# A two-layer hybrid mixer on one core: projection stage's affine steps on another engine, attention's column sums beside its value products, window masks in one format, and the end of layer 0

## The chip, the cores and the metric

The kernel runs on one core of one Trainium2 chip. The time is the device time of one execution in microseconds (us). Before the change it was 2352.65 us, the median of 3 runs (2346.26 to 2353.32).

The engines are named as in the profile: PE is the matrix engine (PEld is its weight loading), DVE the vector engine, ACT the scalar (activation) engine, POOL the general SIMD engine, SP the queue engine that issues most DMA transfers. A "q" behind a name (ACTq, SPq) means the engine's sequencer, for instance when it issues a transfer.

## The reference

Two layers. Each takes 512 latent tokens and 256 context tokens of width 1024, makes one normalised, modulated input `h`, and runs three mixers on it whose outputs are gated and merged:

```
mod = silu(c) @ ada_w + ada_b                     # shift, scale, gate
h = rms_norm(x, norm_g) * (1 + scale) + shift
za, ga, zb, gb, zc, gc, zg = split(h @ w_in)      # 1024 -> 7680 columns, "projection"
# 1. RWKV-7, two directions
z = token_shift(za);  r, k, v, wd, ad = split(z)
decay = exp(-exp(w_log)),  a = sigmoid(a0 + ad @ a_up)
kk = normalised(k * k_k);  k_dir = k * (1 + (a - 1) * k_a)
S <- S diag(w) - (S kk)(kk*a)^T + v k^T;  y = S r # scan over tokens
# 2. latent attention (MLA), dense, 8 heads of 96;  3. windowed GQA, 8 heads of 64,
#    keys within +-128 positions and all context keys, a sink in the softmax
m = sum_n sigmoid(zg_n) * ((y_n * silu(g_n)) @ w_branch_out[n])
x = x + gate * (m @ w_out)
```

The context tokens go through the same layer; of the last layer only the latent output is wanted.

## The kernel before, in words

Everything is float32. A large product is done as three PE products of rounded halves ("fp32r", high and low part of the weights and of the input): `wh*hh`, `wh*hl`, `wl*hh`. The helper `split_w` (L160 to L166) loads four 128x128 weight tiles, makes `wh` on ACT (L165) and `wl` on POOL (L166). Attention's scores use fp32r too; its value products (`yps`, `ypc`), its column sums (`sps`) and the transposed maxima (`mxp`) are plain float32 products, which the trace shows as two instructions each. The window's masks are bf16 products of an identity with a matrix of zeros and large negative numbers, accumulated onto the scores.

A list scheduler sets each engine's order when the kernel is built, by priority bands; the band `SERVE` goes first. A pool hands out on-chip places; a tile that takes a place waits until the last user of that place has ended. Each engine, and each DMA queue, works its list strictly in order.

Per layer the stages follow one another, with projections (`g<-hh,wh` and its two companions) spread as filler between the instructions of the later stages:

- *Projection stage* (`zphase`, about 70 to 300 us in layer 0 and 1400 to 1600 in layer 1). It makes RWKV's inputs. Its main loop has four steps `p` of 128 channels. A step projects `rT` and `vT` (gemms into `gc` and `g`, then a token shift: ACT L352, DVE L353 and L355), reverses `vT` on POOL (L439), transposes it on PE, does two small products whose tanh comes from ACT (L461), and then for both directions `d`: an affine step on `th` (POOL, L466), a running sum (DVE scan, L468), two exponentials (`Ep` L472 and `Em` L475 on ACT, one place for `Em`), an affine step for `kd` (POOL, L478), and ten multiplications into `ar` and `bk` on DVE (L479 to L490). At the end of the step `ks` gets the second direction's `kd` added (POOL, L499). The products `pr<-ar,bk` of a step (`inside`, copied out on ACT at L411) come on PE in the next step, after the next `rT` and `vT` gemms. `ada`, the modulation for later, runs beside it (`modps` on PE from `ada_w` tiles).
- *RWKV scan* with its inverses (300 to 700 us).
- *MLA heads* (about 780 to 960) and *GQA heads* (1010 to 1160 in layer 0). `turns` lets the preparation of one head run beside the attention of the head before. `together` (L857) takes the probability tiles in batches of three and issues their value products; `normalise` (L896) copies the value sum out (ACT, L900), makes the column sums `sps` on PE, and then the reciprocal and the product on DVE. `max_rows` (L873) transposes a head's row maxima (`mxp`).
- *End of the layer*. `gate_out`, called by `gated`, (its transfers are L795, its product L799) loads a gate tile `gt`, multiplies and stores to `ygd`; `branch` (L1334) loads `ygt` from `ygd`, splits it into `yh`/`yl` and multiplies by `w_branch_out`.

Of the kernel before, what the change touches and what calls it, by code (L numbers as in the profile page):

```python
# [60 lines left out]
def build(tc, A, out):  # L61
# [36 lines left out]
    kbias = cpool.tile([P, 3], F32, name="kbias")  # L98
# [3 lines left out]
    b_eps, b_gn, b_kk = kbias[:, 0:1], kbias[:, 1:2], kbias[:, 2:3]  # L102


    win = cpool.tile([P, 3, P], BF16, name="win")
    V.tensor_copy(win[:, 0], ident)
    G.memset(win[:, 1:3], 0.0)
    G.affine_select(win[:, 1], win[:, 1], [[1, P]], ALU.is_ge, NEG, base=0, channel_multiplier=-1)
    G.affine_select(win[:, 2], win[:, 2], [[-1, P]], ALU.is_ge, NEG, base=0, channel_multiplier=1)
# [114 lines left out]
    def ada(l, pp, mod, parts, pool=None):  # L224
# [6 lines left out]
        def bank(shape, name):  # L231
            if pool:
                return rps.tile(shape, F32, tag="c", name=name, bufs=CB)
            return gps.tile(shape, F32, tag="m", name=name, bufs=1)
# [15 lines left out]
        for q, h in [(q, h) for q in parts for h in range(512 // n)]:  # L250
            ps = bank([P, n], "modps")
# [11 lines left out]
            pt = bank([P, nf, 2], "modpt")  # L263
# [79 lines left out]
    def zphase(l, D, hh, hl, last, DL, ready, pace):  # L343
# [18 lines left out]
        with tc.tile_pool(name="zp", bufs=1, reuse_waits="tile") as rp:  # L362
# [36 lines left out]

            def inside():  # L400
# [22 lines left out]
            for p in range(4):  # L423
# [39 lines left out]
                for d in range(2):  # L463

                    th, tha = ths[d], thas[d]
                    G.tensor_scalar(th, th, 0.5, 0.5, ALU.mult, ALU.add)  # L466
                    cum = tmp()
                    V.tensor_tensor_scan(cum, chunk, th, 0.0, ALU.mult, ALU.add)  # L468
                    Ep = big("Ep", [P, NCH, 65], 2)
                    G.memset(Ep[:, :, 0:1], 1.0)  # L470
# [7 lines left out]
                    G.tensor_scalar(kd, tha, c1("ka1"), c1("ka0"), ALU.mult, ALU.add)  # L478
# [19 lines left out]
                    if d:  # L498
                        G.tensor_tensor(ks, ks, kd, ALU.add)  # L499
# [357 lines left out]
    def together(late, values, begins, rest=False):  # L857


        while len(late) >= (1 if rest else EB - 3):  # L860
            some = [late.pop(0) for _ in range(min(len(late), 3))][::-1]
            with band(SERVE), in_line():
                for x in sorted(some, key=lambda x: not begins(*x)):
                    values(*x)

# [5 lines left out]

    def max_rows(mx, r0, nt, row, out, floor=None):
# [3 lines left out]
        mm(ps[rows], mx, ident)  # L876
# [18 lines left out]
    def normalise(ap, yps, acc, n, y, sink=None):  # L895
# [24 lines left out]
    def weigh(o, v, e, c0, first, done):  # L920
# [119 lines left out]
    def mla_heads(l, last, ap, qt, kt, vh, scale, tq0, filler):  # L1040
# [7 lines left out]
        heads, ys, later, late, sums = {}, {}, [], [], {}  # L1048

        def values(hd, k, s0, n, e, acc, y):  # L1050
# [4 lines left out]
            if i == nk - 1:  # L1055
                later.append(normalise(ap, sums.pop((hd, s0))[0], acc[:, s0 - qo:s0 + n - qo], n,
                                       y[:, hd % 2, (s0 - qo) // 2:(s0 + n - qo) // 2]))
                next(later[-1])
                if s0 and hd % 2:
                    later.append(gated(ap, l, 4 + hd // 2, y, segs))  # L1060

        def prepare(hd):
# [25 lines left out]
            max_rows(mx[:, 0, tq0:6], 96, nt, row, qh[xr])  # L1088
            heads[hd] = kh, kl, qh, ql

        def attend(hd):
# [7 lines left out]
            for s0, n, k in [(s0, n, k) for s0, n in segs[::-1] for k in range(6 if s0 else 2)]:  # L1099
# [6 lines left out]
                together(late, values, lambda *x: True)  # L1106
                if s0:
                    yield
            if hd == 7:
                together(late, values, lambda *x: True, True)  # L1110
# [113 lines left out]
    def gqa_heads(l, F, last, ap, KA, KB, vh, sink8, queries, xs, filler):  # L1224
# [8 lines left out]
        ys, sinks, later, qs_, late, sums = {}, {}, [], {}, [], {}  # L1233

        def values(hd, k, g0, s0, e, acc, y):
# [4 lines left out]
            if i == nk - 1:  # L1240
                later.append(normalise(ap, sums.pop((hd, g0))[0], acc[:, g0 - qo:g0 + n - qo], n,
                                       y[:, hd % 2, (g0 - qo) // 2:(g0 + n - qo) // 2],
# [418 lines left out]
```

## Time and profile before

| | us |
|---|---|
| median of 3 runs | 2352.65 |
| profiled execution | 2353.25 |
| its span, first to last instruction | 2351.5 |
| outside the span | 1.75 |
| mean granted PE clock | 0.950 of full |

The profiled execution lies 0.6 us above the median. Sums below are made against its 2353.25. The rows are shown under a heading of their own further down. In a row of a timeline the columns are start, duration, engine, line and operation, output<-inputs, and in brackets the idle time of the engine just before with what ended it. A matrix instruction's duration is longer than its distance to the next one, since they overlap: what an instruction costs is read from one start to the next start.

### The profile page before, as it was taken

To read this page: it belongs to the slowest core of one execution; us is meant where nothing else is said; L and a number is where in the kernel's file an instruction comes from. 1 tells how busy PE (TensorE), PEld (TensorE's weight loads), DVE (VectorE), ACT (ScalarE), POOL (GpSimd) and SP (SyncE) were. 2 spreads that over 40 slices of the span, in tenths; PEclk is the share of its full clock that TensorE was granted. 3 is DMA by queue.
4 is the path that set the end of the run, shared out by engine and by line. 5 is a ranking of instruction groups with operands and counts; after the bars stand their busy time and mean duration, and the time that the engine had idled before them with its cause. 6 is when DMAs were issued, how large, how long until landed. Compare 5 with 4: busy or idle time off the path is not lost. (4 is left out here: it accounts for less than half of the span.)

```text
span 2351.5 us, 42314 instructions
## 1 busy us (share of the span) xinstructions
PE 2096.9 (89%) x16680; PEld 1623.2 (69%) x16680; DVE 1267.4 (54%) x2300; ACT 890.7 (38%) x1654; POOL 865.6 (37%) x699
## 2 busy tenths in 40 slices
PE   6986898888989999989699998889878998999989
PEld 3865676776877766766478876668657876666657
DVE  4476315547436666337537255742668357565643
ACT  3543212233346333354232245433333455534422
POOL 1355312111122344444362324554211145455663
PEclk9998899898999999999899999999989998999999
DMA  7146566554242111431173413566554262215344
GB/s 254 59 137 185 174 201 200 131 144 127 85 132 75 57 41 52 155 121 46 51 238 126 146 61 92 162 201 189 147 127 122 74 215 82 82 50 188 104 156 140
DMA packets 321223, 301.63 MB, mean 128 GB/s; under 512 B 111744, under 2 KB 234368, under 8 KB 321024
## 3 DMA queue, kind: packets, MB, share of 16 engines
q1 hardware_dynamic: 303216, 269.29, 38.3%
q10 hardware_dynamic: 17808, 29.63, 3.9%
q8 instruction: 132, 2.16, 0.4%
q14 instruction: 67, 0.55, 0.1%
HBM read 207.34 MB, written 91.49 MB: 127 GB/s over the span
## 5 line engine op out<-in xcount | busy, mean ns | idle before, releaser
L166 POOL TENSOR_TENSOR wl<-wf,wh 128x512 fp32r<-128x512 f32 x316 | 423.7, 1342 | 999.9 <-ACT wh L165 915.9
L154 PE MATMUL g<-hh,wh 128*128 128x512 f32 (+1 forms) x1264 | 469.2, 372 | 14.5 <-DVE st L782 6.3
L154 PE MATMUL g<-hh,wl 128*128 128x512 f32 (+1 forms) x1264 | 456.1, 361 | 4.1 <-POOL wl L166 4.0
L154 PE MATMUL g<-hl,wh 128*128 128x512 f32 (+1 forms) x1264 | 455.0, 360 | 0.0
L165 ACT CAST wh<-wf 128x512 fp32r<-128x512 f32 x316 | 195.2, 619 | 447.4 <-PE g L154 216.3
L154 PEld LDWEIGHTS g<-hh,wh 128*128 128x128 f32 x1264 | 248.9, 197 | 63.2 <-issue 10.8
L154 PEld LDWEIGHTS g<-hh,wl 128*128 128x128 f32 x1264 | 249.0, 197 | 43.6 <-issue 7.6
L154 PEld LDWEIGHTS g<-hl,wh 128*128 128x128 f32 x1264 | 249.2, 197 | 37.0 <-issue 8.8
L892 POOL TENSOR_TENSOR acc<-acc,pe 128x512 f32<-128x512 f32 (+2 forms) x128 | 145.2, 1135 | 118.0 <-ACT pe L888 98.6
L888 ACT ACTIVATE pe<-stp 128x256 f32<-128x256 f32 (+2 forms) x224 | 114.5, 522 | 190.4 <-PE stp L154 180.2
L870 DVE TENSOR_REDUCE mx<-mps 128x1 f32<-128x384 f32 (+2 forms) x256 | 124.8, 533 | 60.8 <-PE mps L154 60.1
L154 PE MATMUL g<-yh,wh 128*128 128x512 f32 (+1 forms) x224 | 79.3, 357 | 21.4 <-ACT yh L1345 17.7
L154 PE MATMUL yps<-pe,vh 128*64 128x256 f32 (+1 forms) x704 | 95.8, 381 | 1.3 <-ACT tb L900 1.2
L912 DVE RECIPROCAL rec<-sps 128x256 f32<-128x256 f32 (+1 forms) x48 | 70.3, 1478 | 35.3 <-PE sps L154 35.1
L645 DVE TENSOR_TENSOR AR<-scps,cst 64x256 f32<-64x256 f32 x96 | 40.1, 418 | 88.6 <-PE scps L154 87.4
L892 POOL TENSOR_TENSOR acc<-pe 128x512 f32<-128x512 f32 (+1 forms) x48 | 53.2, 1109 | 89.8 <-ACT pe L888 84.3
L154 PE MATMUL g<-yl,wh 128*128 128x512 f32 (+1 forms) x224 | 80.8, 361 | 5.7 <-POOL yl L1346 5.7
L154 PE MATMUL gc<-hh,wh 128*128 128x512 f32 x192 | 76.8, 400 | 8.7 <-ACT hh L325 4.6
L154 PE MATMUL g<-yh,wl 128*128 128x512 f32 (+1 forms) x224 | 79.0, 356 | 0.0
L154 PE MATMUL gc<-hl,wh 128*128 128x512 f32 x192 | 78.1, 407 | 0.1
L154 PE MATMUL scps<-AR,BK 64*128 64x128 f32 (+1 forms) x768 | 63.0, 291 | 15.8 <-DMA AR<-ard 13.5
L679 DVE TENSOR_TENSOR inv<-inv,YB 128x30 f32<-128x30 f32 (+9 forms) x180 | 70.2, 390 | 10.7 <-issue 5.1
(388 smaller groups left out, 4352.6 us busy)
## 6 DMA issues: line engine op xcount, KB each, us to landing
wf<-w_in SPq DMA_DIRECT2D x163, 256.0 KB, 2.9
wf<-ada_w SPq DMA_DIRECT2D x84, 256.0 KB, 4.2
wf<-w_in ACTq DMA_DIRECT2D x77, 256.0 KB, 3.0
bkd<-bk SPq DMA_DIRECT2D x16, 768.0 KB, 6.4
zt<-thzg SPq DMA_DIRECT2D x48, 256.0 KB, 3.1
wf<-w_bo SPq DMA_DIRECT2D x40, 256.0 KB, 2.8
thzg<-st SPq DMA_DIRECT2D x24, 384.0 KB, 2.4
vd<-t SPq DMA_DIRECT2D x64, 96.0 KB, 2.4
```

Of the source, the lines that this page charges most:

```text
L154: queued(TE.matmul(o, l, r, start=start, stop=stop, **kw))
L165: S.copy(wh, w32)
L166: eng.tensor_tensor(wl, w32, wh.bitcast(F32), ALU.subtract)
L645: V.tensor_tensor(AR[oth, pds, 2 * par, :], ps[oth, :, a0:a0 + 64], msk("ms", oth), ALU.mult)
L679: V.tensor_tensor(t3, M3[:, j:j + 1, 0:j].to_broadcast([P, n, j]), YK[:, j + 1:32, j:j + 1].to_broadcast([P, n, j]), ALU.mult)
L870: V.tensor_reduce(mx, ps, AX.X, ALU.max)
L888: S.activation(e, st, AF.Exp, scale=scale)
L892: G.tensor_tensor(acc, keep.pop(0, acc), e, ALU.add)
L912: V.reciprocal(rec, sps)
```

## The change

Six parts.

1. The window's masks become fp32r: two matrices, the identity and one triangle `far`; the other triangle comes from exchanging the two operands. The mask product stays 128x128.
2. `ada` takes one PSUM bank in two halves for its `modps`, and the small transposed product `pt` goes into the same place that the row came from.
3. `zphase`: both affine steps (`th`, `kd`) go from POOL to ACT, the add `ks+kd` from POOL to DVE. The two `Ep` tiles are made once, with their column of ones.
4. Attention: `normalise` stops once more before its reciprocal; the column sums `sps` are issued right behind the next batch of value products (`due`, `close`).
5. `max_rows` multiplies fp32r tiles: the maxima are copied into the last columns of a zeroed tile (`mr`), so that the product has 70 to 102 columns of which the first are zero.
6. `branch` takes its first `ygt` tile before `yh`/`yl`, which in layer 0 have two tags instead of two places of one tag.

```diff
-    win = cpool.tile([P, 3, P], BF16, name="win")
+    win = cpool.tile([P, 2, P], F32R, name="win")
+    identr = win[:, 0]
...
+    windows = {True: (identr, win[:, 1]), False: (win[:, 1], identr)}
...
-                            mm(w[...], win[:, 0], win[:, 1 if k < t else 2],
+                            mm(w[...], *windows[k < t], start=False,
...
         def bank(i):
             if pool:
                 return rps.tile([P, n], F32, tag="c", name="modps", bufs=CB)
+            if not m2:
+                m2.append(gps.tile([P, 512], F32, tag="m", name="modps", bufs=1))
+            return m2[0][:, 256 * (i % 2):256 * (i % 2) + n]
...
-            pt = bank([P, nf, 2], "modpt")
+            pt = ps[:, 0:2 * nf].rearrange("p (f c) -> p f c", c=2)
...
-                    G.tensor_scalar(th, th, 0.5, 0.5, ALU.mult, ALU.add)
+                    S.activation(th, th, AF.Identity, bias=b_half, scale=0.5)
...
-                    Ep = big("Ep", [P, NCH, 65], 2)
-                    G.memset(Ep[:, :, 0:1], 1.0)
+                    Ep = Eps[d]
...
-                    G.tensor_scalar(kd, tha, c1("ka1"), c1("ka0"), ALU.mult, ALU.add)
+                    S.activation(kd, tha, AF.Identity, bias=c1("ka0"), scale=c1("ka1"))
...
-                        G.tensor_tensor(ks, ks, kd, ALU.add)
+                        V.tensor_tensor(ks, ks, kd, ALU.add)
...
-    def together(late, values, begins, rest=False):
+    def together(late, values, begins, due, later, rest=False):
+        def close(ended):
+            for x in ended:
+                next(x[0])
+            later.extend(y for x in ended for y in x)
         while len(late) >= (1 if rest else EB - 3):
+            ended = due[:]
+            due.clear()
             some = [late.pop(0) for _ in range(min(len(late), 3))][::-1]
             with band(SERVE), in_line():
                 for x in sorted(some, key=lambda x: not begins(*x)):
                     values(*x)
+                close(ended)
...
+    def max_columns(ap, r0, nt):
+        mrs = [ap.tile([P, r0 + nt], F32R, name=f"mr{i}") for i in range(2)]
+        for mr in mrs:
+            S.activation(mr, ones[:, 0:1].to_broadcast([P, r0 + nt]), AF.Copy, scale=0.0)
+        return mrs
+    def rounded(mr, mx):
+        V.tensor_copy(mr[:, mr.shape[1] - mx.shape[1]:], mx)
+        return mr
...
-        mm(ps[rows], mx, ident)
+        mm(ps[0:r0 + nt], mx, identr)
...
+        yield
         rec = ap.tile([P, 256], F32, tag="rec", name="rec", bufs=2)[:, 0:h]
...
             if i == nk - 1:
-                later.append(normalise(...))
-                next(later[-1])
+                norm = normalise(...)
+                next(norm)
+                due.append([norm] + ([gated(...)] if s0 and hd % 2 else []))
...
+        yts = [tp.tile([P, 512], F32, tag="ygt", name="ygt", bufs=2 if l else 4)]
-        yh, yl = ({s0: tp.tile([P, 4, n], F32R, tag=f"{t}{s0}", name=t, bufs=1 if l else 2) for (s0, n) in segs}
+        yh, yl = ({s0: tp.tile([P, 4, n], F32R, tag=f"{t}{s0}{0 if l else n_ % 2}", name=t, bufs=1) for (s0, n) in segs}
```

What the change does to the order is seen on two engines. On POOL, in layer 0's projection stage, the list of before has between one `vT` reversal (L439) and the next the two `th` steps (L466), the two `kd` steps (L478), the small fills of `Ep` and the add (L499), with the weight splits `wl` (L166) among them:

```order
L439 TENSOR_SCALAR t_1649<-vT 128x256
L466 TENSOR_SCALAR t_1683<-t_1683 128x768
L466 TENSOR_SCALAR t_1684<-t_1684 128x768
L478 TENSOR_SCALAR ks<-t_1685,der 128x768
L478 TENSOR_SCALAR t_1744<-t_1686,der 128x768
L166 TENSOR_TENSOR wl<-wf,wh 128x512
L470 MEMSET Ep 128x12
L499 TENSOR_TENSOR ks<-ks,t_1744 128x768
L166 TENSOR_TENSOR wl<-wf,wh 128x512
L470 MEMSET Ep 128x12
L166 TENSOR_TENSOR wl<-wf,wh 128x512 x2
L439 TENSOR_SCALAR t_1972<-vT 128x512
```

The same stretch of POOL's list after the change, and some rows on to both sides:

```order
L451 TENSOR_SCALAR t_1322<-vT 128x256
L169 TENSOR_TENSOR wl<-wf,wh 128x512 x4
L451 TENSOR_SCALAR t_1641<-vT 128x512
L451 TENSOR_SCALAR t_1641<-vT 128x256
L169 TENSOR_TENSOR wl<-wf,wh 128x512 x4
L451 TENSOR_SCALAR t_1960<-vT 128x512
```

Only the reversals and the weight splits are left on POOL.

ACT's list in that stage, one step of before (`Ep` is L472, `Em` L475, the token shift's first part L352, weight halves `wh` L165):

```order
L472 ACTIVATE Ep<-t_1389 128x12x64
L475 ACTIVATE Em<-t_1389 128x768
L472 ACTIVATE Ep<-t_1413 128x12x64
L165 CAST wh<-wf 128x512
L162 DMA wf<-w_in 128x512
L352 ACTIVATE rT<-g,der 128x256
L475 ACTIVATE Em<-t_1413 128x768
L165 CAST wh<-wf 128x512
L352 ACTIVATE rT<-gc,der 128x512
L246 DMA wf<-ada_w 128x2x256 x2
```

and the same of after (`th` step L478, `Ep` L483, `Em` L486, `kd` step L489, shift L360, weight halves L168):

```order
L483 ACTIVATE Ep_858<-t_1385 128x12x64
L168 CAST wh<-wf 128x512
L486 ACTIVATE Em<-t_1385 128x768
L165 DMA wf<-w_in 128x512
L489 ACTIVATE ks<-t_1358,der 128x768
L478 ACTIVATE t_1357<-t_1357,kbias 128x768
L168 CAST wh<-wf 128x512
L360 ACTIVATE rT<-gc,der 128x512
L360 ACTIVATE rT<-g,der 128x256
L254 DMA wf<-ada_w 128x2x256
L489 ACTIVATE t_1413<-t_1359,der 128x768
L483 ACTIVATE Ep_859<-t_1407 128x12x64
```

The second direction's `Ep` now stands behind the next step's two `rT` copies, which wait for PE's gemms; before, it stood right behind the first direction's `Em`, and the second direction's `Em` between the two copies.

On PE, near the end of layer 0's GQA heads, before (`sps` are the column sums, `stp` the scores, `win` the masks):

```order
L154 MATMUL yps<-pe,vh 64x256 x2
L154 MATMUL ypc<-pe,vh 64x128 x4
L154 MATMUL mxp<-cst,mx 6x128
L154 MATMUL stp<-QA_8719,KA 128x384
L154 MATMUL stp<-QB,KB 128x384
L154 MATMUL sps<-acc,cst 64x256 x2
L154 MATMUL sps<-er,cst 64x128 x4
L154 MATMUL sps<-acc,cst 64x128 x2
L154 MATMUL sps<-er,cst 64x128 x2
L154 LDWEIGHTS win
L154 MATMUL stp<-win 128x128
```

and the same place after:

```order
L157 MATMUL yps<-pe,vh 64x256 x2
L157 MATMUL ypc<-pe,vh 64x128 x4
L157 MATMUL sps<-acc,cst 64x256 x2
L157 MATMUL sps<-er,cst 64x128 x4
L157 MATMUL mxp<-win,mr_8692 70x128
L157 MATMUL stp<-QA_8685,KA 128x384
L157 MATMUL stp<-QB,KB 128x384
L157 MATMUL stp<-win 128x128 x2
```

The float32 products now stand in one run, and the masks have no weight load of their own in the list.

## Rows read from the trace of the kernel before

**Rows 1.** The page's busy time of each engine, share of the span, instructions.

```profile
PE 2096.9 (89%) x16680; PEld 1623.2 (69%) x16680; DVE 1267.4 (54%) x2300; ACT 890.7 (38%) x1654; POOL 865.6 (37%) x699
```

**Rows 2.** Windows: start:end, length, each engine's busy us, granted clock, DMA share, GB/s.

```profile
120.00:300.00 180.00, 145.00 (x1078) 108.99 (x1079) 101.55 (x150) 60.37 (x113) 80.62 (x51) 0.89 0.57 168
1420.00:1600.00 180.00, 149.41 (x1059) 114.86 (x1059) 101.64 (x128) 78.41 (x135) 93.45 (x66) 0.92 0.55 161
960.00:1160.00 200.00, 184.68 (x1220) 134.56 (x1218) 103.96 (x189) 91.15 (x204) 87.99 (x89) 0.99 0.31 96
```

**Rows 3.** Groups by line, 120 to 300 us: busy us, mean ns | idle before, releaser.

```profile
L468 DVE TENSOR_TENSOR_SCAN t<-chunk,t 128x768 f32<-128x768 f32 x8 | 15.6, 1982 | 21.5 <-POOL t L466 21.5
...
L479 DVE TENSOR_TENSOR t<-t,kT 128x768 f32<-128x768 f32 x4 | 3.8, 946 | 0.0
...
L472 ACT ACTIVATE Ep<-t 128x768 f32<-128x768 f32 x8 | 6.8, 848 | 6.4 <-POOL wl L166 4.6 <-DVE t L468 1.6
```

**Rows 4.** One line's instructions: the add L499; durations in ns, minimum/median/maximum.

```profile
L499 POOL TENSOR_TENSOR ks<-ks,t x8: 2449/5890/6219, 144.6 to 1565.0; 128x768 f32<-128x768 f32 x8
```

**Rows 5.** Timeline, layer 0, step 2 of the projection stage, all engines.

```profile
170.80 1.99 POOL L166 TENSOR_TENSOR wl<-wf,wh 128x512 fp32r<-128x512 f32 x1
171.57 1.77 DVE L485 TENSOR_TENSOR ar<-kkn,Ep 128x512 f32<-128x512 f32 x1
...
177.52 6.20 POOL L499 TENSOR_TENSOR ks<-ks,t 128x768 f32<-128x768 f32 x1 [1.52 <-DVE t L479]
...
178.23 0.68 DVE L485 TENSOR_TENSOR ar<-kkn,Ep 128x512 f32<-128x512 f32 x1
...
183.68 1.26 POOL L166 TENSOR_TENSOR wl<-wf,wh 128x512 fp32r<-128x512 f32 x1
...
189.66 1.07 PE L154 MATMUL modps<-wf,sc 128*32 128x256 f32 x4 [12.20 <-DMA wf<-ada_w]
```

**Rows 6.** Timeline of PE: two more of its gaps in the projection stages.

```profile
238.47 0.80 PE L154 MATMUL pr<-ar,bk 64*64 64x64 f32 x10 [8.15 <-ACT t L411]
...
1468.07 1.23 PE L154 MATMUL pr<-ar,bk 64*64 64x64 f32 x18 [6.93 <-DVE bk L488]
```

**Rows 7.** What the tile `modps` waited for on PE: us, times.

```profile
  DVE mod L272: 6.8, 4
```

**Rows 8.** Timeline of PE in layer 0's GQA heads.

```profile
1141.31 0.28 PE L154 MATMUL mps<-win 128*128 128x128 bf16 x2
...
1141.99 0.23 PE L154 MATMUL mps<-win 128*128 128x128 bf16 x1
1142.03 0.37 PE L154 MATMUL stp<-QA,KA 128*128 128x256 f32 x1
1142.23 0.28 PE L154 MATMUL stp<-QB,KB 128*128 128x256 f32 x1
1142.36 0.23 PE L154 MATMUL stp<-win 128*128 128x128 bf16 x1
...
1143.54 0.38 PE L154 MATMUL mxp<-cst,mx 128*6 128x128 f32 x2
1143.85 0.45 PE L154 MATMUL stp<-QA,KA 128*128 128x384 f32 x1
1144.14 0.34 PE L154 MATMUL stp<-QB,KB 128*128 128x384 f32 x1
1144.40 0.65 PE L154 MATMUL sps<-acc,cst 128*64 128x256 f32 x4
```

**Rows 9.** Groups of PE's weight loads by form, 960 to 1160 us.

```profile
L154 PEld LDWEIGHTS stp<-QB,KB 128*128 128x128 f32 x64 | 12.3, 192 | 0.2
...
L154 PEld LDWEIGHTS <-win 128*128 128x128 bf16 x96 | 6.8, 97 | 6.2 <-issue 3.4
```

**Rows 10.** Timeline of SP's queue at layer 0's end.

```profile
1171.14 1.24 SPq L795 DMA_DIRECT2D ygd<-gt  x2
1173.90 1.76 SPq L1344 DMA_DIRECT2D ygt<-ygd  x4
```

More of the change, by code (lines that the diff above doesn't have):

```diff
@@ L97, in build @@
     ident, bones, ones = C["ident"], C["bones"], C["ones"]
-    kbias = cpool.tile([P, 3], F32, name="kbias")
+    kbias = cpool.tile([P, 4], F32, name="kbias")
     V.memset(kbias[:, 0:1], EPS)
@@ L229, in ada, with bank @@
         n = 512 if pool else 256
-        def bank(shape, name):
+        m2 = []
+        def bank(i):
             if pool:
-                return rps.tile(shape, F32, tag="c", name=name, bufs=CB)
-            return gps.tile(shape, F32, tag="m", name=name, bufs=1)
+                return rps.tile([P, n], F32, tag="c", name="modps", bufs=CB)
+            if not m2:
+                m2.append(gps.tile([P, 512], F32, tag="m", name="modps", bufs=1))
+            return m2[0][:, 256 * (i % 2):256 * (i % 2) + n]
         def four(q, h, k0):
@@ L248, in four @@
             return [ws[i // 2][:, i % 2] for i in range(4)]
-        for q, h in [(q, h) for q in parts for h in range(512 // n)]:
-            ps = bank([P, n], "modps")
+        for i_, (q, h) in enumerate((q, h) for q in parts for h in range(512 // n)):
+            ps = bank(i_)
             for k0 in range(0, KT, 4):
@@ L398, in zphase @@
             late, sums = [], []
+            Eps = [big(f"Ep{d}", [P, NCH, 65]) for d in range(2)]
+            for Ep in Eps:
+                G.memset(Ep[:, :, 0:1], 1.0)
             def inside():
@@ L864, in together @@
                     values(*x)
+                close(ended)
+        if rest:
+            with in_line():
+                close(due)
+            due.clear()
     def max_tile():
@@ L1047, in mla_heads @@
             S.copy(kh[xr, :], ones[xr, 0:1].to_broadcast([nt, T]))
-        heads, ys, later, late, sums = {}, {}, [], [], {}
+        mrs = max_columns(ap, 96, nt)
+        heads, ys, later, late, sums, due = {}, {}, [], [], {}, []
         def values(hd, k, s0, n, e, acc, y):
@@ L1105, in attend @@
                 late.append((hd, k, s0, n, probs(ap, st, n, scale, acc[:, sl], k, keep, EB), acc, y))
-                together(late, values, lambda *x: True)
+                together(late, values, lambda *x: True, due, later)
                 if s0:
@@ L1109, in attend @@
             if hd == 7:
-                together(late, values, lambda *x: True, True)
+                together(late, values, lambda *x: True, due, later, True)
         turns(8, prepare, attend, later, filler)
@@ L1232, in gqa_heads @@
         segs = (LAT,) if last else (LAT, CTX)
-        ys, sinks, later, qs_, late, sums = {}, {}, [], {}, [], {}
+        mrs = max_columns(ap, 64, nt)
+        ys, sinks, later, qs_, late, sums, due = {}, {}, [], {}, [], {}, []
         def values(hd, k, g0, s0, e, acc, y):
@@ L1240, in values @@
             if i == nk - 1:
-                later.append(normalise(ap, sums.pop((hd, g0))[0], acc[:, g0 - qo:g0 + n - qo], n,
-                                       y[:, hd % 2, (g0 - qo) // 2:(g0 + n - qo) // 2],
-                                       (sinks[hd][xr], xr, xr.start - tq0 + g0 // P)))
-                next(later[-1])
-                if g0 and hd % 2:
-                    later.append(gated(ap, l, 8 + hd // 2, y, segs))
+                norm = normalise(ap, sums.pop((hd, g0))[0], acc[:, g0 - qo:g0 + n - qo], n,
+                                 y[:, hd % 2, (g0 - qo) // 2:(g0 + n - qo) // 2],
+                                 (sinks[hd][xr], xr, xr.start - tq0 + g0 // P))
+                next(norm)
+                due.append([norm] + ([gated(ap, l, 8 + hd // 2, y, segs)] if g0 and hd % 2 else []))
         def begins(hd, k, g0, *_):
@@ L1317, in attend @@
                 st = rps.tile([P, 512], F32, tag="r", name="stp", bufs=RB)[:, 0:n]
-                edges = [(t * P - s0, 1 if t < k else 2) for t in range(s0 // P, s1 // P) if t != k] if k >= 2 else []
+                edges = [(t * P - s0, windows[t < k]) for t in range(s0 // P, s1 // P) if t != k] if k >= 2 else []
                 mm(st, KA[:, kv, ks], QA[:, s0 - qo:s1 - qo], stop=False, skip_group_check=bool(edges))
@@ L1321, in attend @@
                 for e, (o_, w) in enumerate(edges):
-                    mm(st[:, o_:o_ + P], win[:, 0], win[:, w], start=False, stop=(e == len(edges) - 1),
+                    mm(st[:, o_:o_ + P], *w, start=False, stop=(e == len(edges) - 1),
                        skip_group_check=True)
                 late.append((hd, k, g0, s0, probs(ap, st, n, scale, acc[:, s0 - qo:s1 - qo], k, keep, EB), acc, y))
-                together(late, values, begins)
+                together(late, values, begins, due, later)
                 if g0:
```

31 lines of the change are left out of this document (16 added, 15 removed).

## The prediction, made before the changed kernel ran

> **What bounds the kernel now.** I read the page's busy times first: PE is busy for 2096.9 us, 89% of the span, DVE for 54%, ACT and POOL for under 40% [rows 1]. So where PE is full, an edit is worth what it takes off PE, and where PE idles, what shortens the chain that PE waits for. The windows tell the two kinds of stage apart [rows 2]: in the GQA stage PE is busy for 184.68 of 200 us at a granted clock of 0.99, while in the two projection stages it is busy for 145.00 and 149.41 of 180 us, at 0.89 and 0.92. These two hold 35.0 + 30.6 = 65.6 us of PE idle time, and the first, third and fourth part of the change fall on the one kind or the other. Then I read, in the idle stages, the timeline around PE's gaps, and in the full ones the distances from one PE start to the next.
>
> **Projection stage (parts 2 and 3).** Removed from POOL: 16 `th` steps, 16 `kd` steps, 8 adds. Added: 32 ACT instructions of 768 columns, which I price by the exponential of the same size, 0.85 us [rows 3], 27 us in all, and 8 DVE adds at the 0.95 us of the product of that size [rows 3], 7.6 us. POOL's add took 2.4 to 6.2 us, 5.9 in the median [rows 4].
>
> ACT's 27 us cost nothing as such: it is busy for 60.37 of the 180 us in layer 0 [rows 2]. In the chain an affine step on ACT stands where one on POOL stood. The adds are another matter, because of what is queued behind them. At 177.52 POOL begins the add, which lasts 6.20 us. The weight split `wl` behind it in POOL's list starts only at 183.68; it gives a staging place free, ACT's queue issues the `ada_w` load when it has ended, and PE, which waits for that load, has stood for 12.20 us when it goes on at 189.66 [rows 5]. After the change POOL has nothing between two reversals of `vT` but weight splits, so the split can start where the add did. That takes 6.2 us out of this chain and puts 0.95 in (the DVE add): 5.2. The next step of layer 0 has the same long add, and its PE gap of 8.15 us ends with an ACT copy that waits in the same list [rows 6]; I count 5.2 again. Together 10.4.
>
> In the other six steps the add is shorter or nobody waits for it; PE's gap of 6.93 us in layer 1 ends with DVE's `bk` [rows 6], that is with the chain on DVE. That chain is stretched while POOL works: one and the same 512-column product took 1.77 us beside a POOL split and 0.68 beside the add [rows 5], 1.1 us apart. The scan waits 21.5 us in layer 0 for POOL's `th` step [rows 3], but most of that is the tanh before it, which stays. I take 1.1 for the stretch and 1.1 for the wait on `kd` and the second stretched product of a step, less 0.95 for the new add: 1.3 us a step, 8 for six. Sum for the stage: 18. Its ends are 0, if ACT's longer list delays the second direction as much as POOL is relieved, and the whole 65.6 of idle time.
>
> On this the Trainium skill has a rule (SBUF — State Buffer, "Who interferes with whom"): DVE and POOL share a pair of ports as an exclusive lock, and the loser waits for the whole instruction of the other. The 1.77 us agree with it: the POOL split began at 170.80 and lasted 1.99, to 172.79, and 0.68 later is 173.47, where the product ended at 173.34 [rows 5]. By that rule the weight splits, which stay on POOL, go on blocking DVE, and now start earlier in the step, while DVE works on `ar` and `bk`; the 1.1 of the stretch would not come back, and the stage would give 10.4 + 6 x 0.2 = 11.6 instead of 18.
>
> `ada`: PE waited 6.8 us for the `mod` addition before it could begin the next `modps` [rows 7]. With halves of a bank it need not. Most of that time PE then waits for the next load instead; I take 2, between 0 and 6.8.
>
> **Attention (parts 1, 4, 5).** First the order. Scores are fp32r, sums and values float32, and every passage from one to the other costs PE time that the starts show: a 256-column score product has the next start 0.13 behind it, unrounded about 0.12, so one of 384 columns should take 0.18; the one followed by `sps` takes 0.26, and the one that follows `mxp` 0.29, some 0.09 more for a passage in either direction [rows 8]. Counted in the two lists, the attention stages of both layers have 276 passages before and 176 after, since sums, values and `mxp` now stand in one run. 100 x 0.09 = 9 us off PE, where PE is full. That the reciprocal and the product come later costs nothing as long as the next head covers them; the order leaves a batch at least.
>
> `mxp` as float32 takes two instructions, 0.31 us to the next start, passage included [rows 8], 0.22 without; as one fp32r instruction 0.11 to 0.22. 32 of them: 0 to 3.5 saved; I take 3. The 32 small DVE copies stand before it and lie beside scores.
>
> The masks: 192 products of 128 columns, 64 alone and 64 pairs. In bf16 the mask costs PE little: after it the next product starts 0.04 later and that one lasts 0.20 instead of 0.13, 0.12 for a mask with its return to fp32r [rows 8]; two in a row last 0.28 where one lasts 0.23, so the second of a pair starts 0.05 to 0.065 behind the first. What an fp32r product of under 256 columns costs no row of before shows. From below, it is the 256 columns' 0.13 at most halved; but the weights must be loaded, and an fp32r load of 128 columns lasts 192 ns against 97 for bf16 [rows 9], and no fp32r product with its load follows another closer than the 0.12 of those with 256 columns. So 0.12 each: nothing for those alone, 0.055 for each pair, +3.5 us. From above, it is the float32 price, 0.213 for 128 columns (the 0.22 of `mxp`): 64 x 0.095 + 64 x 0.243 = +21.7; and if it were also to pay the passage both ways, 128 x 0.19 = 24 more, +45.7. I take +3.5, since the rows nearest to it are fp32r products, whose price goes with columns down to the load.
>
> The Trainium skill speaks against the masks' new format (TensorE: Matmul & The Clock Gate, "Weight-path perf modes"): the fast weight load is on for 128 weights of a type that isn't FP32. The loads' 97 against 192 ns agree [rows 9]. By that rule alone each mask pays the longer load in full where nothing covers it, 192 x 0.095 = 18 instead of 3.5, and the whole would come to 2337.
>
> Attention in sum: -9 - 3 + 3.5 = -8.5.
>
> **Layer 0's end (part 6).** The last two stores are issued from 1171.14 for 1.24 us, to 1172.38, but the `ygt` loads behind them in SP's list only at 1173.90 [rows 10]: the first of them has the place of `gt`, so it waits for the stores to land. In the list of after it waits for PE alone and can go 1.52 earlier: -1.5. They stay behind these stores in SP's list, so the long wait of PE there (from the ping-pong of one `gt` tile) stays.
>
> **Sum.** -18 - 2 - 8.5 - 1.5 = -30 from the profiled 2353.25, 2323.25; the median lies 0.6 lower: 2323.
>
> **Rivals.**
> (a) An fp32r product of 128 columns costs as much as float32: masks +21.7, `mxp` 0. Attention +12.7, in all -9: 2344. For it speaks that the kernel has no such product under 256 columns; against it that price went with columns in all forms seen.
> (b) ACT takes POOL's place. The second direction's `Ep` stands behind two `rT` copies that wait for PE's gemms of the next step (the orders show it); the stage gains nothing: -12, 2341. For it: DVE had its scan's result used at once before. Against: ACT idles for two thirds of the stage [rows 2], and `wl` comes earlier, thus the gemms too.
> (c) Slower: each mask group pays the float32 price and the passage both ways, in GQA's scores, +45.7 against -30.5 of all the rest (`mxp` 0): +15, 2368. It decides from 30.5/128 = 0.24 us for a group above today's price, where nothing is left of the gain.
> (d) The end of layer 0 is not moved, or is later: in SP's new list a gate store that waits for ACT stands among the `gt` transfers; +3, about one of the store-to-load distances there (1171.14 to 1173.90 [rows 10]), instead of -1.5: 2327.
>
> **How the numbers follow.** The forecast 0.50, (a) 0.20, (b) 0.15, (c) 0.10, (d) 0.05. The forecast's own range is 2304 (the projection stages give half of their idle time back, 33) to 2338. The range that should hold 8 in 10 goes from 2300 to 2354: it holds (a), (b) and (d) and leaves (c) out. A difference of under 0.3%, 7 us, can't be told from none here. Faster by more: 0.95 of the forecast and (d), half of (a), 0.75 of (b): 0.73. The rest of (a) and (b) is no change, with a little of the forecast, 0.13; (c) and what I may have missed, 0.14.
>
> **What would show it.** Right: PE busy in the two projection windows at over 155 of 180 us, no gap of 12 us before `modps`, no POOL work there but splits and reversals; in GQA the mask 0.11 to 0.13 from start to start, and no 0.09 before `sps`; `ygt` issued within 1.5 us of the last store. Wrong: masks 0.2 apart (then (a) or (c)), PE's gaps in the projection stage ending with ACT's `Ep` (then (b)).

## The result, and the profile after

The changed kernel took 2327.84 us (median of 4 runs, 2322.13 to 2331.07), beside 2350.17 for the kernel before, 22 us less by these medians. The ratio is 0.9885, 95% interval 0.986 to 0.9911, which is 27 us. Run again later beside the experiments, on a chip where the kernel before took 2357.17, it took 2327.81, a ratio of 0.9881 (0.986 to 0.9901). So it is faster by 22 to 29 us; 2323, 30 less, was forecast. The sum came out near, partly because errors of its terms cancel.

A table of stages, each from one PE start to another in the profiled executions, the last one to PE's end (us):

| from ... to | before | after | after, again |
|---|---|---|---|
| start ... last `pr<-ks`, layer 0 | 288.0 | 284.6 | 285.8 |
| of it the loop, from the first `pr<-twd` | 161.7 | 151.2 | 151.0 |
| RWKV, to the first MLA score | 496.9 | 498.7 | 497.9 |
| MLA, GQA, end of layer 0, to the first `g<-yh` | 392.6 | 378.3 | 377.2 |
| branch, head, projection of layer 1 | 414.5 | 409.2 | 408.0 |
| of it the loop | 148.6 | 141.6 | 141.6 |
| RWKV, layer 1 | 422.6 | 418.8 | 421.5 |
| MLA, GQA, tail of layer 1 | 333.3 | 330.9 | 332.2 |

The two last columns are the same kernel, and its stages differ by up to 3 us. Among the runs below the spread is wider. Nine runs have the same PE list in layer 0's loop and nearly the same in layer 1's; the loops took 145.7 to 151.2 us and 140.5 to 145.2 in them. RWKV differs by up to 8 with nearly the same list. So nothing under 7 us is read from one stage of one run alone. Both loops together lost 17.5 us, 18 was forecast for the stage. But layer 0's loop begins 7 us later than before (133.3 against 126.3), and attention lost 16.7 where 10 were forecast with the end of layer 0.

The page's busy line [rows 1]:

```profile
PE 2080.5 (90%) x16648; PEld 1631.0 (70%) x16648; DVE 1271.3 (55%) x2342; ACT 920.2 (40%) x1694; POOL 787.7 (34%) x646
```

POOL lost 78 us; ACT gained 30, where 27 were priced; PE lost 16. The windows of [rows 2], the same stretches of time:

```profile
120.00:300.00 180.00, 149.66 (x1111) 112.49 (x1110) 103.57 (x160) 80.78 (x138) 42.50 (x27) 0.91 0.58 174
1420.00:1600.00 180.00, 155.66 (x1115) 119.75 (x1114) 95.94 (x133) 86.95 (x153) 63.39 (x44) 0.96 0.63 180
960.00:1160.00 200.00, 170.54 (x1143) 132.32 (x1143) 109.96 (x200) 84.98 (x194) 81.79 (x80) 0.95 0.29 92
```

PE is busier in both projection stages, though the sign that the prediction gave, over 155 of 180 us, holds in the second alone. POOL works half as long in the first. The third window now holds the idle end of the layer, which begins earlier. What became of the gap of 12.20 us [rows 5] and of that of 8.15 [rows 6], in the timeline of PE:

```profile
184.91 0.63 PE L157 MATMUL modps<-wf,sc 128*32 128x256 f32 x4 [1.46 <-DMA wf<-ada_w]
190.96 0.62 PE L157 MATMUL modps<-wf,sc 128*32 128x256 f32 x4 [1.95 <-DMA wf<-ada_w]
...
199.58 0.64 PE L157 MATMUL modps<-wf,sc 128*32 128x256 f32 x2 [3.06 <-DMA wf<-ada_w]
...
235.92 1.12 PE L157 MATMUL pr<-ar,bk 64*64 64x64 f32 x16 [6.48 <-ACT t L423]
...
271.83 1.07 PE L157 MATMUL modps<-wf,sc 128*32 128x256 f32 x4 [5.50 <-DMA wf<-ada_w]
```

The loop's waits for `ada_w` are now four short ones, 12.0 us together; before they were three, 13.3 together, with the long one among them. Step 2, which had the long one, has three of the four with 6.5 us, so 5.7 less; the fourth, 5.50, is in the last step. The gap of 8.15 is now 6.48. In GQA the place of [rows 8]:

```profile
1124.24 0.33 PE L157 MATMUL mps<-win 128*128 128x128 f32 x2
1124.41 0.45 PE L157 MATMUL mps<-KB,QB 128*128 128x256 f32 x2
1124.70 0.22 PE L157 MATMUL mps<-win 128*128 128x128 f32 x1
1124.76 0.33 PE L157 MATMUL stp<-QA,KA 128*128 128x256 f32 x1
1124.93 0.28 PE L157 MATMUL stp<-QB,KB 128*128 128x256 f32 x1
1125.05 0.22 PE L157 MATMUL stp<-win 128*128 128x128 f32 x1
1125.26 0.65 PE L157 MATMUL yps<-pe,vh 128*64 128x256 f32 x4
1125.74 0.61 PE L157 MATMUL ypc<-pe,vh 128*64 128x128 f32 x8
1126.18 0.60 PE L157 MATMUL sps<-acc,cst 128*64 128x256 f32 x4
1126.71 0.65 PE L157 MATMUL sps<-er,cst 6*64 6x128 f32 x8
1127.46 0.25 PE L157 MATMUL mxp<-win,mr 128*70 128x128 f32 x1
1127.55 0.39 PE L157 MATMUL stp<-QA,KA 128*128 128x384 f32 x1
```

Values, sums and maxima stand in one run. A mask alone has the next start 0.06 behind it and that product takes 0.17, 0.23 together (0.24 in bf16 [rows 8]); a pair takes 0.17 to the next start, and the two 256-column products behind it 0.29 where two take 0.24. The first of the two behind the pair takes 0.17 as well: part of a mask's price shows in the product behind it, in both formats. Neither the float32 price nor a passage is paid: rivals (a) and (c) are out by these rows alone. The transposed maxima take 0.09 instead of 0.31.

The weight loads, by form [rows 9]; the masks' are now as long as the scores':

```profile
L157 PEld LDWEIGHTS stp<-QB,KB 128*128 128x128 f32 x64 | 12.2, 190 | 0.4 <-issue 0.3
L157 PEld LDWEIGHTS mps<-win 128*128 128x128 f32 x48 | 8.8, 188 | 0.1
```

And SP's queue at the end of layer 0 [rows 10]:

```profile
1156.39 1.24 SPq L806 DMA_DIRECT2D ygd<-gt  x2
1157.67 2.03 SPq L1386 DMA_DIRECT2D ygt<-ygd  x4
```

The loads start 1.28 behind the stores and not 2.76: the 1.5 of the forecast, to the tenth.

### The profile page after: what moved, and what is told of

It is laid out like the page before. It is cut to its first block, busy times and chain, and to the rows that moved or that the text cites. A ratio compares the mean times of both kernels' runs of the same rounds, so it can differ in the third digit from the quotient of the medians.

```text
span 2324.2 us, 42281 instructions
## 1 busy us (share of the span) xinstructions
PE 2080.5 (90%) x16648; PEld 1631.0 (70%) x16648; DVE 1271.3 (55%) x2342; ACT 920.2 (40%) x1694; POOL 787.7 (34%) x646
## 5 line engine op out<-in xcount | busy, mean ns | idle before, releaser
L169 POOL TENSOR_TENSOR wl<-wf,wh 128x512 fp32r<-128x512 f32 x316 | 439.7, 1393 | 1129.4 <-ACT wh L168 1068.6
L168 ACT CAST wh<-wf 128x512 fp32r<-128x512 f32 x316 | 195.1, 619 | 422.2 <-PE g L157 190.0
L157 PEld LDWEIGHTS g<-hh,wh 128*128 128x128 f32 x1264 | 249.8, 198 | 59.2 <-issue 10.4
L157 PE MATMUL gc<-hh,wh 128*128 128x512 f32 x192 | 78.9, 411 | 10.1 <-DVE rT L363 5.6
L157 PE MATMUL gc<-hh,wl 128*128 128x512 f32 x192 | 76.5, 399 | 0.0
```

The lines of the kernel that those rows point to most:

```text
L157: queued(TE.matmul(o, l, r, start=start, stop=stop, **kw))
L168: S.copy(wh, w32)
L169: eng.tensor_tensor(wl, w32, wh.bitcast(F32), ALU.subtract)
```

## The experiments

All ratios are to the kernel before, timed on the same chip; the changed kernel's own is 0.9881 to 0.9885. Edits are shown against the changed kernel.

**The head's banks.** The table shows that layer 0's loop begins late, and the PE list of the head has its modulation products in single pieces. Timeline of PE before, in the head, the first batches (columns as before; an instruction count of 2 is one float32 product):

```profile
36.82 1.91 PE L154 MATMUL modps<-wf,sc 128*32 128x512 f32 x12
...
39.76 1.04 PE L154 MATMUL modps<-wf,sc 128*32 128x512 f32 x2
```

and after:

```profile
35.67 1.04 PE L157 MATMUL modps<-wf,sc 128*32 128x512 f32 x2
...
37.78 1.05 PE L157 MATMUL modps<-wf,sc 128*32 128x512 f32 x2
...
40.44 1.05 PE L157 MATMUL modps<-wf,sc 128*32 128x512 f32 x4
```

Each of the four products of a batch writes a quarter of the rows (128*32); alone one takes 1.04 us, six in a row 1.91. Two kernels test this.

```diff
-            pt = ps[:, 0:2 * nf].rearrange("p (f c) -> p f c", c=2)
+            pt = (rps.tile([P, nf, 2], F32, tag="c", name="modpt", bufs=CB) if pool else
+                  ps[:, 0:2 * nf].rearrange("p (f c) -> p f c", c=2))
```

> The changed kernel with one thing undone: in the head of layer 0, where the modulation products have 512 columns, the small transposed product has a bank of its own again. Theory: with both in one bank the modulation products come free earlier, each goes as its own weights land, and what were runs of four that overlap on PE become single ones; that is why their PE time in the head rose from 14.9 us (9 runs) to 21.4 us (16 runs). Undone, they take about 15 us again, the first step of the projection stage's loop begins some 6 us earlier (at 127 instead of 133 us), and the whole comes to about 2322. Rival: the head's order was changed by something else (the Ep tiles, the masks' set-up); then the runs stay 16 and the time 2328.

2320.22 us, ratio 0.9853 (0.9831 to 0.9875). The products took 15.1 us of PE from start to next start in 9 runs (before 14.9 in 9, after 21.4 in 16), and the loop began at 128.2. In the second the batch is issued last weights first:

```diff
-                    for i in range(4):
+                    for i in reversed(range(4)):
                         mm(ps[32 * i:32 * i + 32], sc2[:, k0 + i, :], ws[i], start=(k0 == 0), stop=(k0 + 4 == KT),
```

> The changed kernel, and in the modulation product the four products of a batch are issued last first, so that the first of them waits for the weights that land last and the other three follow at once. Theory (overlap of the four is what counts): all runs in the head are of four, PE time of these products 14 us or less instead of 21.4, whole time 2321. Rival (PE waits for the weights anyway, and what counts is when they land): the head stays as long, or a batch that waits holds back the projections behind it, time 2328 or more.

2323.78 us, ratio 0.9866 (0.9841 to 0.9891). All batches are whole, timeline of PE:

```profile
41.52 1.80 PE L157 MATMUL modps<-wf,sc 128*32 128x512 f32 x8
45.66 1.06 PE L157 MATMUL modps<-wf,sc 128*32 128x512 f32 x8
50.00 1.07 PE L157 MATMUL modps<-wf,sc 128*32 128x512 f32 x8
```

Four products in 1.06 us, as long as one alone; 10.0 us in all. But PE waits for the last weights: up to the end of the loop it idles 11 us more than in the changed kernel, and between 30 and 60 us the granted clock is 0.78 in place of 0.94. The time can't be told from that of the banks, nor from the changed kernel's. The theory holds for PE's time and the loop's start: the bank's wait of before had kept the batches together, and taking it away broke them up. In time the banks alone are worth 7 us, at the edge of the noise; beside bf16 masks (below) they are clear of it.

**The projection stage.**

```diff
-                    S.activation(th, th, AF.Identity, bias=b_half, scale=0.5)
+                    G.tensor_scalar(th, th, 0.5, 0.5, ALU.mult, ALU.add)
...
-                    S.activation(kd, tha, AF.Identity, bias=c1("ka0"), scale=c1("ka1"))
+                    G.tensor_scalar(kd, tha, c1("ka1"), c1("ka0"), ALU.mult, ALU.add)
...
-                        V.tensor_tensor(ks, ks, kd, ALU.add)
+                        G.tensor_tensor(ks, ks, kd, ALU.add)
```

> The changed kernel with both affine steps and the add of the projection stage back on POOL. Theory of the prediction: this part was worth 18 us; in the trace the loop from the first lora product to the last bonus product fell from 161.7 to 151.2 us in layer 0 and by some 7 in layer 1. So 2345, the 12 us gap before the modulation product is back, and attention stays as in the changed kernel. Rival: the loop is paced by weights' transfers, and its gain comes from the banks of the modulation or from another order; then 2328 to 2334.

2355.75 us, ratio 0.9999 (0.9986 to 1.0013). The loops took 164.7 and 149.0 us, 20.9 more than in the changed kernel together; of the 27 us in all the other 6 lie in stages with the same or nearly the same lists. The 12 us gap is back, timeline of PE:

```profile
200.58 1.07 PE L157 MATMUL modps<-wf,sc 128*32 128x256 f32 x4 [12.18 <-DMA wf<-ada_w]
```

and of POOL in the same step:

```profile
176.90 3.11 POOL L489 TENSOR_SCALAR ks<-t,der 128x768 f32<-128x768 f32 x1 [0.80 <-ACT t L473]
179.99 1.80 POOL L489 TENSOR_SCALAR t<-t,der 128x768 f32<-128x768 f32 x1
181.75 1.99 POOL L169 TENSOR_TENSOR wl<-wf,wh 128x512 fp32r<-128x512 f32 x1
188.46 6.20 POOL L510 TENSOR_TENSOR ks<-ks,t 128x768 f32<-128x768 f32 x1 [4.72 <-DVE t L490]
194.62 1.26 POOL L169 TENSOR_TENSOR wl<-wf,wh 128x512 fp32r<-128x512 f32 x1
```

Two weight splits stand behind POOL's own work: the first behind the `kd` steps, the second behind the add. The first waited 0.8 us there after its `wh` was ready, the second 5.8. The second ends the gap: it is done at 195.88, ACT's queue issues the `ada_w` loads at 195.91, and PE goes on at 200.58. That is the chain of the prediction. The next kernel has the last of the three edits alone.

> The changed kernel with only the add of ks and kd back on POOL (the affine steps stay on ACT). All of the third part was worth 27 us by the run that undid it. Theory of the prediction: the add stands ahead of the weight splits and carries 10 of 18, so here some 15 of 27: 2343, a ratio to the kernel before of 0.995. Rival: what counts is that DVE's chain no longer runs beside POOL's affine steps and doesn't wait for them, and the add alone, of 2.5 to 6 us and off DVE's chain, costs 0 to 5: ratio 0.989 to 0.991.

2335.59 us, ratio 0.9906 (0.9883 to 0.993). Loops 154.1 and 144.4, 5.7 longer together, and the time 6 us; neither is clear of the spread. So the add alone is worth some 6 us or nothing, and the other 15 of the loops come back only with the affine steps on POOL too. The long add is there, and the split behind it late, but the splits before it are early (timeline of POOL):

```profile
174.59 1.75 POOL L169 TENSOR_TENSOR wl<-wf,wh 128x512 fp32r<-128x512 f32 x1 [8.13 <-ACT wh L168]
179.62 1.78 POOL L169 TENSOR_TENSOR wl<-wf,wh 128x512 fp32r<-128x512 f32 x1 [3.27 <-ACT wh L168]
185.87 6.31 POOL L510 TENSOR_TENSOR ks<-ks,t 128x768 f32<-128x768 f32 x1 [4.47 <-DVE t L490]
192.14 1.26 POOL L169 TENSOR_TENSOR wl<-wf,wh 128x512 fp32r<-128x512 f32 x1
```

The gap of 12 us isn't back (PE's waits for `ada_w` are four, 11.7 us, as in the changed kernel). The theory's 15 is out; the rival's number holds. But the add has not become harmless: the lists differ. With the affine steps on ACT the scheduler sets the casts `wh` of the next weights earlier on ACT, so that the split which stood behind the add in the kernel above, at 194.62, runs ahead of it here, at 179.62. In both loops together, splits whose `wh` was ready stood for 32.9 us behind adds and 11.8 behind affine steps in the kernel above, and for 7.1 behind adds here. The affine steps alone on POOL, with the add on DVE, weren't run. Then the affine steps on a third engine:

```diff
-                    S.activation(th, th, AF.Identity, bias=b_half, scale=0.5)
+                    V.tensor_scalar(th, th, 0.5, 0.5, ALU.mult, ALU.add)
...
-                    S.activation(kd, tha, AF.Identity, bias=c1("ka0"), scale=c1("ka1"))
+                    V.tensor_scalar(kd, tha, c1("ka1"), c1("ka0"), ALU.mult, ALU.add)
```

> The changed kernel with both affine steps on DVE in place of ACT, so that POOL is as free as in the changed kernel and DVE has 32 more instructions of 768 columns, some 0.5 to 0.9 us each, 16 to 28 us. Theory (what counted was POOL's list, in which the weight splits stood behind the affine steps): the loop of the projection stage stays near its 151 us in layer 0 and 142 in layer 1, at most 5 longer, ratio 0.988 to 0.992. Rival (the chain on DVE is the pace, and what counted was that it neither waits for POOL nor shares its port): the loop goes back to 160 and more, ratio 0.996 to 1.0.

2337.01 us, ratio 0.9916 (0.9884 to 0.9948). Loops 154.7 and 142.2, 4 us longer together, though DVE has 32 more instructions. So the chain on DVE didn't set the pace. What did was the work on POOL, by what stands behind it there or by the order that the scheduler gives the other engines beside it; these runs don't part the two.

**The sums.** `normalise` without its new stop, and appended to `later` as before:

```diff
-        yield
         rec = ap.tile([P, 256], F32, tag="rec", name="rec", bufs=2)[:, 0:h]
...
-                due.append([norm] + ([gated(...)] if s0 and hd % 2 else []))
+                later.extend([norm] + ([gated(...)] if s0 and hd % 2 else []))
```

> The changed kernel with the column sums issued as before, by normalise at the next flush and not beside the next values. Theory of the prediction: 100 passages between the formats are back, 9 us; but the trace shows 14 us less in layer 0's attention and more than 11 in layer 1's MLA, so that sums whose two halves stand apart may cost further 3 to 5: 2337 to 2341. Rival (the gain is that of the maxima's product and of other order): 2331 or less.

2345.72 us, ratio 0.9951 (0.9932 to 0.997). The attention stages of both layers took 724.4 us in place of 709.2, PE 16 us busier. The list has 248 passages against 176: 72 at 0.09 are 6.5, not 15. The price of a passage varies: 34 places where a score or a projection is followed by `sps` cost 4.3 us over that product's own distance, some 0.09 and some 0.19; the changed kernel has 3 such places, 0.5 us. Most of the difference stands in the float32 products themselves: from start to next start the sums take 47.7 us against 40.3, the value products 98.1 against 91.9.

**Masks and maxima.** Masks in bf16 again (a small fp32r identity stays for the maxima):

```diff
-    windows = {True: (identr, win[:, 1]), False: (win[:, 1], identr)}
+    windows = {True: (winb[:, 0], winb[:, 1]), False: (winb[:, 1], winb[:, 0])}
```

> The changed kernel with the window masks in bf16 again. The trace of the changed kernel has a mask's next start 58 to 62 ns behind it and the pair's second 113, so theory: the masks in fp32r cost 64 x 0.045 for the pairs and save 0.017 for those alone, +2 us, at most +6 by the distances around them; undone 2322 to 2326, a ratio of 0.986 to 0.988. Rival (a) of the prediction (float32 price): -22, ratio 0.979.

2323.84 us, ratio 0.9844 (0.9825 to 0.9862), better by 9 than the changed kernel; 2 to 6 were expected. From start to next start the 192 masks took 12.5 us against 19.5 in the changed kernel and 13.1 before, but that isn't the price of the format, since the product behind a bf16 mask takes longer. Counted with that product, whose own distance is taken off, a mask alone costs 0.13 us in either format, a pair 0.26 in fp32r and 0.18 in bf16 (means). For 64 pairs that is 5 us, within what was expected. The rest is in layer 1: there 8.9 us of branch products that fill GQA in bf16 are left over for the tail in fp32r. The list scheduler, which sees other durations, puts them there, and the tail has 5 us more idle time (10.3 against 5.3). Layer 1's attention and tail together are 8 us shorter here than in the changed kernel, and about 7 or 8 in the two kernels with bf16 masks below. This is where part of attention's gain went: layer 1's last sum starts 37.9 us earlier than before, the kernel ends 27.5 earlier.

Maxima as a float32 product, in MLA (shown) and in GQA:

```diff
-        mm(ps[0:r0 + nt], mx, identr)
+        mm(ps[rows], mx, ident)
...
-            max_rows(rounded(mrs[hd % 2], mx[:, 0, tq0:6]), 96, nt, row, qh[xr])
+            max_rows(mx[:, 0, tq0:6], 96, nt, row, qh[xr])
```

> The changed kernel with the row maxima transposed as before by a float32 product with the maxima as weights, without the copy into a zeroed tile. Theory of the prediction: +3 us (32 times 0.1), ratio 0.990. Rival: each float32 product between scores also has a passage in and out, 32 x 0.19 = 6 more where no other float32 product stands beside it, together up to +9.5: ratio 0.9925.

2320.69 us, ratio 0.9839 (0.9812 to 0.9866): neither expected rise came. The maxima's own PE time is 4.5 us after and was 10.1 before, so the product did get cheaper, yet undoing it costs no time. In layer 0 projections of 8.7 us then stand in the gap at the layer's end, where PE idles 13.4 instead of 17.1. That fillers placed elsewhere make up for the product fits this, but isn't shown: attention is only 4.7 us shorter here, and layer 0's attention took 373.5 us in the run with bf16 masks and 379.7 with one and the same list in the first run below.

**Versions that beat both.** The banks and bf16 masks together, then with the maxima too:

> A version that may beat both: the changed kernel with the bank of its own for the head's transposed product (ratio 0.985 alone) and the masks in bf16. If the two are independent: -7 and -2 to -6 from 2328, 2315 to 2319, ratio 0.983 to 0.985. If bf16 masks bring nothing: as with the banks alone, 0.985.

2309.78 us, ratio 0.9786 (0.977 to 0.9803).

> The best version by the single runs: the changed kernel with three edits undone (a bank of its own for the head's transposed product, masks in bf16, maxima as a float32 product). If the gains add: 0.9786 with the first two, and 5 to 10 us more with the third: 0.974 to 0.977. If the maxima's gain was that of where the fillers fell (the end of GQA in layer 0 kept 8.7 us of projections for its gap), it need not add: 0.978 to 0.981.

2304.35 us, ratio 0.9783 (0.9762 to 0.9804); beside it on the same chip the changed kernel:

> The changed kernel itself once more, beside the others on one chip, so that differences of 5 us can be told: ratio 0.9885 as at first. If the earlier ratio was an accident of the chip, 0.985 to 0.992, and the differences of the single edits (banks 7, masks 10, maxima 11 us better than the changed kernel by their ratios) shrink or grow by as much.

2327.81 us, 0.9881. So the first two add up within the noise, and the maxima add nothing that can be told; only 1.9 us of projections stand in the gap at layer 0's end here. The last version keeps the third, fourth and sixth part of the change and half of the second, and is 1% faster than the whole change.

**The place at layer 0's end.**

```diff
-        yts = [tp.tile([P, 512], F32, tag="ygt", name="ygt", bufs=2 if l else 4)]
+        yts = []
```

> The changed kernel without the early first tile of the branch, so that this tile has the place of gt again. Theory of the prediction: the loads wait for the last stores to land, +1.5 us, to be seen in the queue as 1.5 between the last store and the first load. The trace of the changed kernel has PE's gap at the end of layer 0 only 0.6 shorter, so the rival: 0.6 or nothing in the time, since the loads' data come from the stores' own queue; ratio 0.9885 to 0.989.

2332.45 us, ratio 0.99 (0.9882 to 0.9918), no difference that can be told from the changed kernel. SP's queue:

```profile
1161.77 1.24 SPq L806 DMA_DIRECT2D ygd<-gt  x2
1163.05 2.03 SPq L1386 DMA_DIRECT2D ygt<-ygd  x4
```

The load still stands 1.28 behind the stores: the early tile isn't what freed it. What did (the two tags of `yh` and `yl` are the other edit there) wasn't tried by itself.

## Why the prediction was right, and where it wasn't

**Projection stage, -18.** The size was right: -17.5 between the kernels, 20.9 by undoing the part. By steps, each from its first `pr<-twd` to the next step's, the two with the long adds gave 7.0 and 2.7 us, where 5.2 and 5.2 were forecast; the other six gave 7.9 together, where 8 was (one step with the same list varies by up to 4). The mechanism, weight splits held up in POOL's list, was right too, and undoing the part brings back the chain behind the add as the prediction read it.

Two steps of it don't hold as they stand. The first is "in the chain an affine step on ACT stands where one on POOL stood", which priced the move at nothing: the add alone on POOL brings back some 6 us, not 10.4, and the rest of the loops' 20.9 comes only with the affine steps there too, which change where the casts and the splits stand. The second is that the split behind the add goes on taking its 1.26 us. In step 3 it now starts while DVE works through its products (225.25 to 232.8 without a gap), timeline of POOL:

```profile
225.60 6.33 POOL L169 TENSOR_TENSOR wl<-wf,wh 128x512 fp32r<-128x512 f32 x1 [5.14 <-ACT wh L168]
```

That is as long as the add had been, ACT waited for it 6.9 us, and of the 8.15 us gap 6.48 stayed. The stretch of DVE, which was to give the rest, mostly stayed too: the 120 products into `ar` and `bk` of both loops took 87.7 us before and 82.1 after (66.5 if none were stretched), while the same 33 splits grew from 49.0 to 65.2. What gave the 7.9 us of the six other steps isn't shown. Rival (b) fell: no gap ends with ACT's `Ep`.

**Banks, -2.** Wrong in sign: +6.5 us of PE time in the head. The row that I used [rows 7] is of waits on PE; I took it that a wait removed can cost nothing. It had served to collect four products that overlap. What the halves of a bank gave in the later stages wasn't tried by itself.

**Passages, -9, and maxima, -3.** The sums were worth 15 by undoing; less than half of it is passages at my price. And the price belongs to something else than I took it for. Scores are products of fp32r with weights 128 columns wide (the second figure of 128*128), sums and values of float32 with weights 64 wide (128*64), so format and shape change together there. Where a float32 product on 128*128 stands between fp32r ones, nothing is paid (timeline of PE after, `pr` is plain float32; then a place with `sps`):

```profile
679.73 0.39 PE L157 MATMUL g<-hh,wl 128*128 128x512 f32 x1
679.96 0.59 PE L157 MATMUL pr<-yo,cst 128*128 128x256 f32 x2
680.39 0.59 PE L157 MATMUL pr<-ro,cst 128*128 128x256 f32 x2
680.64 0.58 PE L157 MATMUL g<-hh,wh 128*128 128x512 f32 x1
681.05 0.40 PE L157 MATMUL g<-hl,wh 128*128 128x512 f32 x1
...
843.91 0.50 PE L157 MATMUL stp<-qh,kh 102*128 102x512 f32 x1
844.34 0.65 PE L157 MATMUL sps<-acc,cst 128*64 128x256 f32 x4
844.93 0.50 PE L157 MATMUL stp<-qh,kl 96*128 96x512 f32 x1
845.26 0.40 PE L157 MATMUL stp<-ql,kh 96*128 96x512 f32 x1
```

From 679.96 to 681.05 are 1.09 us, which is two float32 products at 0.43 and one of fp32r at 0.23. The score before `sps` takes 0.43 in place of 0.23, the one behind it 0.33. Within float32 the price is there as well: a sum `sps<-acc` takes 0.31 us where `sps<-er` on 6*64 or 4*64 follows and 0.21 where the next product is on 128*64 too. So the passage is one between shapes, not between formats.

The maxima's product gained 5.6 on PE, more than the 3; in the time nothing of it is seen.

**Masks, +3.5.** Of the bounds the lowest was near: a mask alone costs no more than in bf16, as priced, a pair 0.08 more where 0.055 was priced, 5 us in all. The time moved by 9, in part by where fillers stand in layer 1, which the prediction didn't have. The Trainium skill's rule on the fast weight load (TensorE: Matmul & The Clock Gate, "Weight-path perf modes") agrees with the loads, 188 instead of 97 ns; the 18 us that it would give if nothing covered the load didn't come. Rivals (a) and (c), float32's price, fell.

**Layer 0's end, -1.5.** Right in the queue, 1.48; PE's gap got only 0.6 shorter. From the last sum to the last store it took 12.2 us instead of 11.6; the gate store of rival (d) now stands among the transfers (`thzg`, at 1140.58), though that it is the cause wasn't tried.

So that the whole came near the forecast is in part luck, by two errors that cancel: attention's sums gave 6 more, the head's banks took 8.5 from what I had counted.

## What to carry to other kernels

When work is moved off an engine, look at everything that was queued behind it there, for every instruction moved, and at how the other engines' lists change with it: parts undone one by one need not give back what they gave together. A wait may be doing a service: before removing one, see whether the instructions behind it overlap only when they come together. When a price shows between two kinds of instruction, list all that differs between them and look for a place where only one of these changes. And price an instruction together with the one behind it, and judge an edit on the whole time, since a scheduler may place fillers anew.

## What the runs showed of the hardware

- Four float32 products of 128x32 weights into four quarters of the rows take 1.06 us together where they stand side by side in PE's list, one alone 1.04.
- An fp32r product of 128 columns has the next start 0.06 us behind it, but the 256-column product behind it takes 0.17 in place of 0.12, and the second of two in a row 0.11.
- Going from a product on 128*128 to one on 128*64 or back cost some 0.10 us (at places 0.20) beside the products' own distances; going from fp32r to float32 and back on 128*128 cost nothing.
- A weight split on POOL takes 1.26 us alone; beside an unbroken row of DVE's products it took 6.33 in the changed kernel (above), and 6.69 with the affine steps on DVE, timeline of POOL:

```profile
176.73 6.69 POOL L169 TENSOR_TENSOR wl<-wf,wh 128x512 fp32r<-128x512 f32 x1 [10.35 <-ACT wh L168]
```

The Trainium skill (SBUF — State Buffer, "Who interferes with whom") has the two engines share a pair of ports as an exclusive lock; the rows agree with POOL being shut out for several of DVE's instructions in a row.
